# Score groups on even turns in layer 0's attention, another order and other banks in its output projection, and two weight splits per turn where the feed-forward begins

## The chip, the core and the metric

The kernel runs on one core of a Trainium2 chip. The metric is the device time of one execution in microseconds, from the first to the last instruction and what lies around them. The engines are named as in the profile: PE (TensorE, products and transposes), PEld (its weight loads), ACT (ScalarE), DVE (VectorE), POOL (GpSimd) and SP (SyncE, which issues the loads of the weights).

## What is computed

Two layers of a transformer trunk on 256 tokens of 1024 features. Layer 0 uses a dilated sliding-window attention with three head groups per head (windows 128, 512, 2048 with steps 1, 4, 16), merged by their softmax denominators; layer 1 a block-sparse attention. Each layer ends with a gated feed-forward with a causal convolution of width 3. The reference, cut:

```python
def reference(x, attn_norm, a_w_qkv, ..., ffn_w_down):
    for i in range(DEPTH):                       # 2
        hn = rmsnorm(x, attn_norm[i])
        x = x + (mixer_dilated if i % 2 == 0 else mixer_moba)(hn, w_qkv, q_gain, k_gain, w_o, cos, sin)
        hn = rmsnorm(x, ffn_norm[i])
        x = x + conv_ffn(hn, ffn_w_up[i], ffn_conv_w[i], ffn_conv_b[i], ffn_w_down[i])

def mixer_dilated(h, ...):
    qkv = h @ w_qkv                              # (256, 3 * 3 * 16 * 64)
    q, k = rope(rmsnorm(q)), rope(rmsnorm(k))
    # per head group: scores, mask, softmax, times v; then merged
    return attn @ w_o

def conv_ffn(h, w_up, conv_w, conv_b, w_down):
    u = h @ w_up                                 # (256, 2 * 2816)
    uc = conv_b + sum(conv_w[j] * shifted(u, j) for j in range(3))
    gate, val = uc[..., :D_FF], uc[..., D_FF:]
    return (silu(gate) * val) @ w_down
```

## The kernel before

**Products in three parts.** All is float32. A weight unit is loaded raw (SP), ACT copies it to a shorter type (whi, line 87) and DVE subtracts to get the rest (wlo, line 96). An activation is held in two parts likewise (xT in the profile, lines 372 and 373). A product is then three matmuls: first part times whi, second part times whi, first part times wlo (mm3, lines 384 to 386). Tokens come in two chunks of 128, c = 0 and 1. The `Stream` class holds the queue of weight units: `start` issues whi on ACT, `finish` issues wlo on DVE and the next load, `take` hands units to PE.

**Turns.** The order on each engine is the order in which the program is written, and the program is written in turns (`turn`, line 184). A turn issues up to `pump` whi on ACT, then what is due in `first`, one wlo, what is due in `pre`, the other wlo, then its piece of products for PE, then what is due in `post`. Functions enter themselves for later turns by `at(table, dt, fn)`. Pieces of a product with 12 matmuls of 512 columns make one turn in the attention.

**Attention of layer 0.** Four sections of four heads. A section has, for each of three head groups, four turns for queries and keys (two for chunk 0, then two for chunk 1), then four turns for values; sections 0 and 2 have four more for values. Turns are counted from the start of the section. A product's result sits in a bank named acc (three banks). Queries and keys are scaled, rotated and transposed back (line 473, acc<-ident,qk). The scores of two heads of one chunk are a *score group* (`step_A`, lines 573 and 582, into two banks named S); the table `plan` says after which turn of the section each group stands. One turn later DVE takes maxima with the mask (line 595) and ACT the exponentials (line 605), one more turn later DVE divides (line 615) and PE transposes the result (line 622, two banks named PT), then ACT copies it (pT, line 629) and PE multiplies with the values (line 649, one bank named O). After the second group of a chunk O is split into aT, which has the buffer name xT too (lines 372, 373). In the last section the four groups stand on turns 13 to 16, so their later steps fall into the turns of the output projection. Between islands of such small products PE runs weight products.

**Output projection** (`out_proj`, line 675). Chunk c, half n of the output columns, and weight unit u (rows 256u to 256u+255): eight units in the order `OUT_UNITS`, written (n, u). Unit u needs section u of the attention, and of the last section both chunks, since the attention's tokens are permuted. `OUT_ORDER` lists for each turn the pump, the chunk and the units. Chunk 0 accumulates in acc banks, chunk 1 in S banks:

```python
acc[c, n] = ps.tile([P, 512], F32, name="acc" if c == 0 else "S", bufs=3 - c)
```

When a half is complete it is added to the residual (line 695), squared, and with both halves the chunk's norm is computed and transposed (line 280) into the next activation.

**Feed-forward** (`ffn`, line 713). Eleven blocks of 256 columns in both halves j (gate and value). Block 0 is computed in four turns with the tokens on the partitions and transposed (line 745, into the PT banks). From block 1 on, each turn computes 128 columns of the block for both chunks (24 matmuls of 256 columns, lines 760 to 762). The convolution (`conv`) runs on ACT (line 774) and DVE (line 777); with both halves done, gate times value is split into two parts (kT, lines 786, 787), which the down-projection reads (lines 801 to 803, into the S and PT banks). From block 2 on, each second turn of j = 1 is followed by a down-projection of an earlier block.

## Time and profile before

| | us |
|---|---|
| median of 3 runs | 788.14 |
| lowest and highest run | 788.06, 788.2 |
| the profiled execution's own time | 788.0 |
| its span, first to last instruction | 786.2 |
| PE busy in it | 776.2 |
| DVE busy | 551.2 |
| ACT busy | 480.8 |

The span is 1.8 us shorter than the execution's own time. A row of a timeline has a start and a length. Lengths of PE's products overlap: the next one starts before the last has ended, so the time of a stretch of PE is read from start to start. A group of small products between weight products is called an island here.

### The profile page before, as it was taken

The numbers are of one execution on the slowest core, as the hardware profiler recorded it, in microseconds if no ns is written. First come the engines' busy times: TensorE is split into PE (matmuls) and PEld (weight loads), VectorE is DVE, ScalarE is ACT, GpSimd is POOL, SyncE is SP. The second block draws the span as 40 slices with busy tenths as digits, with TensorE's granted clock in tenths as the row PEclk, the third lists the DMA queues.
The fourth block names the chain that finished last, engine by engine and source line by source line (L and its number), as shares of the span: only waits on it lengthen the run. The fifth ranks groups of instructions, "written<-read, shape, count | busy, mean of one in ns | idle before, by whom it ended". The sixth has DMA issues, their size and how long they took to land.

```text
span 786.2 us, 13306 instructions
## 1 busy us (share of the span) xinstructions
PE 776.2 (99%) x5042; PEld 669.2 (85%) x5042; DVE 551.2 (70%) x1010; ACT 480.8 (61%) x811; POOL 89.3 (11%) x117
## 2 busy tenths in 40 slices
PE   8999999999999999999999999999999999999997
PEld 6888887888887779999999988777778999999996
DVE  6884876785686565887656777787866686676763
ACT  7677576676666546575554655877755565565550
POOL 3720331230231000000000002132100000000000
PEclk9999999999999999999999999999999999999999
DMA  9976436445356425576665563653535467556611
GB/s 292 292 241 209 123 122 188 135 141 182 114 181 214 135 81 165 167 236 209 190 208 167 161 203 120 204 169 109 158 111 183 140 208 242 167 161 193 203 34 53
DMA packets 107919, 133.89 MB, mean 170 GB/s; under 512 B 5968, under 2 KB 92368, under 8 KB 107856
## 3 DMA queue, kind: packets, MB, share of 16 engines
q1 hardware_dynamic: 107280, 130.96, 52.6%
q0 software_dynamic: 576, 2.10, 0.7%
q8 instruction: 39, 0.64, 0.3%
q14 instruction: 24, 0.20, 0.1%
HBM read 131.99 MB, written 1.05 MB: 169 GB/s over the span
## 4 chain that ended last, share of the span: by engine, by line
PE 90%; ACT 4%; DVE 3%; DMA 1%; issue 1%; SPq 0%; DVEq 0%; ACTq 0%
PE acc L384 12%; PE acc L386 12%; PE acc L385 12%; PE acc L762 9%; PE acc L761 9%; PE acc L760 9%; PE S L801 3%; PE S L802 3%; PE S L803 3%; PE PT L801 2%; PE PT L803 2%; PE PT L802 2%; PE O L649 2%; PE PT L622 2%; PE acc L473 2%; PE S L573 2%
## 5 line engine op out<-in xcount | busy, mean ns | idle before, releaser
L96 DVE TENSOR_TENSOR wlo<-raw,whi 128x1024 fp32r<-128x1024 f32 (+1 forms) x248 | 289.5, 1204 | 18.5 <-ACT whi L87 18.5
L87 ACT ACTIVATE whi<-raw 128x1024 fp32r<-128x1024 f32 (+1 forms) x248 | 249.0, 1040 | 17.6 <-PE PT L802 13.9
L384 PE MATMUL acc<-whi,xT 128*128 128x512 f32 x448 | 183.2, 409 | 2.0 <-ACT whi L87 1.3
L762 PE MATMUL acc<-xT,wlo 128*128 128x256 f32 x640 | 181.2, 283 | 0.5 <-DVE wlo L96 0.5
L760 PE MATMUL acc<-xT,whi 128*128 128x256 f32 x640 | 181.1, 283 | 0.0
L761 PE MATMUL acc<-xT,whi 128*128 128x256 f32 x640 | 181.1, 283 | 0.0
L386 PE MATMUL acc<-wlo,xT 128*128 128x512 f32 x448 | 176.0, 393 | 0.6 <-DVE wlo L96 0.5
L385 PE MATMUL acc<-whi,xT 128*128 128x512 f32 x448 | 174.9, 390 | 0.4 <-DVE xT L373 0.2
L761 PEld LDWEIGHTS acc<-xT,whi 128*128 128x128 f32 x640 | 122.7, 192 | 1.3
L760 PEld LDWEIGHTS acc<-xT,whi 128*128 128x128 f32 x640 | 122.7, 192 | 1.3
L762 PEld LDWEIGHTS acc<-xT,wlo 128*128 128x128 f32 x640 | 122.7, 192 | 0.7 <-DVE wlo L96 0.7
L777 DVE SCALAR_TENSOR_TENSOR qk<-acc,pk,qk 128x255 f32<-128x255 f32 (+1 forms) x160 | 66.1, 475 | 72.9 <-ACT qk L774 72.9
L384 PEld LDWEIGHTS acc<-whi,xT 128*128 128x128 f32 x448 | 84.1, 188 | 21.7 <-issue 2.6
L386 PEld LDWEIGHTS acc<-wlo,xT 128*128 128x128 f32 x448 | 84.0, 188 | 21.5 <-DVE wlo L96 3.0
L385 PEld LDWEIGHTS acc<-whi,xT 128*128 128x128 f32 x448 | 84.4, 188 | 16.3 <-DVE xT L373 1.0
L774 ACT ACTIVATE qk<-acc,pk 128x256 f32<-128x256 f32 x80 | 40.6, 558 | 33.0 <-PE acc L762 33.0
L263 POOL TENSOR_TENSOR rs_y<-rs_v,mhalf 128x8 f32<-128x8 f32 x32 | 53.3, 1664 | 2.7
L786 ACT ACTIVATE kT<-qk 128x512 fp32r<-128x512 f32 x22 | 13.9, 632 | 54.8 <-DVE qk L784 54.8
L261 POOL TENSOR_SCALAR rs_v<-qssq,rn_e 128x8 f32<-128x8 f32 x32 | 16.4, 513 | 217.9 <-DVE qssq L436 217.7
L780 ACT ACTIVATE qk<-qk 128x512 f32<-128x512 f32 x22 | 13.9, 633 | 35.6 <-DVE qk L777 35.6
L801 PE MATMUL S<-whi,kT 128*128 128x512 f32 x88 | 34.7, 394 | 0.0
L802 PE MATMUL S<-whi,kT 128*128 128x512 f32 x88 | 34.7, 394 | 0.0
(126 smaller groups left out, 920.0 us busy)
## 6 DMA issues: line engine op xcount, KB each, us to landing
raw<-in_ffn_w_up_dram SPq DMA_DIRECT2D x80, 512.0 KB, 4.6
raw<-in_a_w_qkv_dram SPq DMA_DIRECT2D x144, 256.0 KB, 4.2
raw<-in_ffn_w_down_dram SPq DMA_DIRECT2D x44, 512.0 KB, 5.0
raw<-in_b_w_qkv_dram SPq DMA_DIRECT2D x48, 256.0 KB, 4.0
raw<-in_a_w_o_dram SPq DMA_DIRECT2D x8, 512.0 KB, 4.1
raw<-in_ffn_w_up_dram SPq DMA_DIRECT2D x16, 256.0 KB, 5.5
raw<-in_b_w_o_dram SPq DMA_DIRECT2D x8, 512.0 KB, 3.8
xr<-in_x_t_dram SPq DMA_DIRECT2D x4, 256.0 KB, 5.5
```

Source lines behind the costliest of these rows:

```text
L87: self.nc.scalar.activation(hi[:, i], raw[:, i], AF.Copy)
L96: self.nc.vector.tensor_sub(lo[:, i], self.raw[self.done][:, i], r32(hi[:, i]))
L263: nc.gpsimd.tensor_tensor(y, v, mhalf[:, 0:n], op=ALU.pow)
L384: nc.tensor.matmul(acc, T[:, k, 0, cs], hi, start=first, stop=False)
L385: nc.tensor.matmul(acc, T[:, k, 1, cs], hi, start=False, stop=False)
L386: nc.tensor.matmul(acc, T[:, k, 0, cs], lo, start=False, stop=last)
L760: nc.tensor.matmul(o, hi[:, k % 4, es], xT[:, k, 0], start=(k == 0), stop=False)
L761: nc.tensor.matmul(o, hi[:, k % 4, es], xT[:, k, 1], start=False, stop=False)
L762: nc.tensor.matmul(o, lo[:, k % 4, es], xT[:, k, 0], start=False, stop=(k == 7))
L777: nc.vector.scalar_tensor_tensor(o[:, d:S], u[:, 0:S - d], cw[:, first_tap + b:first_tap + b + 1], o[:, d:S], op0=ALU.mult, op1=ALU.add)
L801: nc.tensor.matmul(o, acts[f][:, 0, cs], hi[:, sl], start=(b == 0), stop=False)
L802: nc.tensor.matmul(o, acts[f][:, 1, cs], hi[:, sl], start=False, stop=False)
```

## The change

Five edits. (1) In sections 0 to 2 of layer 0's attention the two score groups of chunk 0 stand after turns 14 and 18 instead of 13 and 17. (2) `OUT_ORDER` of layer 0 now names chunk and unit for each piece, so a turn may mix chunks; chunk 0's third unit moves into the second turn, and the turns behind have one unit each. (3) In both layers chunk 1's first half accumulates in an acc bank; only its second half goes to S. (4) In the last turns of layer 0's attention (after its turn 12) and in its output projection a turn's second whi is issued behind the functions due in `first` (`crowded`). (5) The turns of the feed-forward's block 1 have a pump of 2 throughout, in both layers.

```diff
-OUT_ORDER = (((1, 0, 0, 1), (1, 1, 0, 1), (2, 0, 2, 3), (0, 1, 2), (1, 0, 4, 5), (0, 0, 6), (0, 0, 7), (0, 1, 3), (1, 1, 4),
-              (1, 1, 5), (0, 1, 6), (0, 1, 7)),
-             tuple((1, 0, u) for u in range(8)) + tuple((int(u < 6), 1, u) for u in range(8)))
+OUT_ORDER = (((1, (0, 0), (0, 1)), (1, (1, 0), (1, 1), (0, 2)), (2, (0, 3)), (0, (1, 2)), (1, (0, 4)), (0, (0, 5)), (0, (0, 6)),
+              (0, (0, 7)), (0, (1, 3)), (1, (1, 4)), (1, (1, 5)), (0, (1, 6)), (0, (1, 7))),
+             tuple((1, (0, u)) for u in range(8)) + tuple((int(u < 6), (1, u)) for u in range(8)))
...
-    def turn(fn, pump=2):
+    def turn(fn, pump=2, crowded=False):
+
         t = now[0]
         end = len(ws.parts) if t >= LATE else None
-        ws.start(min(pump, 1 if len(ws.parts) - ws.taken >= AHEAD else 2))
+        n = min(pump, 1 if len(ws.parts) - ws.taken >= AHEAD else 2)
+        ws.start(min(n, 1) if crowded else n)
         for f, a in first.pop(t, ()):
             f(*a)
+        if crowded:
+            ws.start(n - 1)
         ws.finish(1, end)
...
-            plan = odd = [(13, 0, (0, 1)), (17, 0, (2, 3)), (22, 1, (0, 1)), (26, 1, (2, 3))]
+            plan = odd = [(14, 0, (0, 1)), (18, 0, (2, 3)), (22, 1, (0, 1)), (26, 1, (2, 3))]
...
-                turn(fn, pumps[i] if sec == 0 and i < len(pumps) else 2)
+                turn(fn, pumps[i] if sec == 0 and i < len(pumps) else 2, dil and sec == NSEC - 1 and i > 12)
...
-        def piece(c, *idx):
+        def piece(*idx):
             def go():
-                for n, u in idx:
+                for c, i in idx:
+                    n, u = OUT_UNITS[i]
                     if c == 0:
                         units[n, u] = ws.take(1)[0]
                     _, hi, lo = units[n, u]
                     if u == 0:
-                        acc[c, n] = ps.tile([P, 512], F32, name="acc" if c == 0 else "S", bufs=3 - c)
+                        acc[c, n] = ps.tile([P, 512], F32, name="S" if c and n else "acc", bufs=2 if c and n else 3)
...
-        for pump, c, *us in OUT_ORDER[l]:
-            turn(piece(c, *(OUT_UNITS[u] for u in us)), pump)
+        for pump, *idx in OUT_ORDER[l]:
+            turn(piece(*idx), pump, l == 0)
...
-                    turn(up(f, j, e, st), 1 if f == 1 and (j, e) != (1, 0) else 2)
+                    turn(up(f, j, e, st), 2)
```

In the changed file the functions stand four or five lines lower, so mm3 is lines 388 to 390 there, and so on. The order of the instructions shows what moves.

PE in section 0 of layer 0's attention, around the first score group (S; t are the queries and keys of the second and third head group). Before it stands alone:

```order
L386 MATMUL acc<-wlo,xT 128x512
L573 MATMUL S<-kT 128x256 x6
L582 MATMUL S<-t_505 64x64 x2
L582 MATMUL S<-t_639 64x64 x4
L582 MATMUL S<-t_505 64x64 x2
L384 MATMUL acc<-whi,xT 128x512
L385 MATMUL acc<-whi,xT 128x512
```

Now:

```order
L390 MATMUL acc<-wlo,xT 128x512
L577 MATMUL S<-kT 128x256 x6
L586 MATMUL S<-t_505 64x64 x2
L586 MATMUL S<-t_639 64x64 x4
L586 MATMUL S<-t_505 64x64 x2
L477 MATMUL acc<-ident,qk 128x128 x4
L388 MATMUL acc<-whi,xT 128x512
```

The group stands one turn later, in front of the transposes of the third head group of chunk 1. Counted over the whole program, PE has 87 islands between weight products before and 80 now; in layer 0's attention seven pairs have become one.

PE behind the last O group of layer 0 (pT_3164). acc_3028 and acc_3130 (before) or acc_3100 (now) are the two halves of chunk 0; whi_3003 is unit (0, 3), the first that needs the last section, and whi_2953 is unit (1, 2), which was whi_2940 before. Before:

```order
L386 MATMUL acc_3130<-wlo_2941,xT_180 128x512
L649 MATMUL O_3174<-pT_3164,v1_2868 64x128 x2
L649 MATMUL O_3174<-pT_3164,v2_2320 64x64 x4
L649 MATMUL O_3174<-pT_3164,v1_2968 64x128 x2
L384 MATMUL acc_3028<-whi_3003,xT_180 128x512
L385 MATMUL acc_3028<-whi_3003,xT_180 128x512
L386 MATMUL acc_3028<-wlo_3004,xT_180 128x512
```

Now:

```order
L390 MATMUL acc_3028<-wlo_2938,xT_180 128x512
L653 MATMUL O_3174<-pT_3164,v1_2868 64x128 x2
L653 MATMUL O_3174<-pT_3164,v2_2316 64x64 x4
L653 MATMUL O_3174<-pT_3164,v1_2968 64x128 x2
L388 MATMUL acc_3100<-whi_2953,xT_180 128x512
L389 MATMUL acc_3100<-whi_2953,xT_180 128x512
L390 MATMUL acc_3100<-wlo_2954,xT_180 128x512
L388 MATMUL acc_3100<-whi_2953,xT_180 128x512
L389 MATMUL acc_3100<-whi_2953,xT_180 128x512
L390 MATMUL acc_3100<-wlo_2954,xT_180 128x512
L388 MATMUL acc_3028<-whi_3003,xT_180 128x512
L389 MATMUL acc_3028<-whi_3003,xT_180 128x512
```

Unit (1, 2) of chunk 0 stood ahead of the O group and stands behind it now; the six products of chunk 0's unit (1, 0) moved from the third turn into the second in exchange.

DVE where layer 0's feed-forward begins, from the second weight parts ahead of the first convolution: the convolutions of block 0's gate (out of PT), block 1's gate (out of acc) and block 0's value (out of PT), then gate times value (qk<-qk) and its second part (kT). Before:

```order
L96 TENSOR_TENSOR wlo<-raw,whi 128x1024 x5
L777 SCALAR_TENSOR_TENSOR qk<-PT,pk,qk 128x255 x2
L777 SCALAR_TENSOR_TENSOR qk<-PT,pk,qk 128x254 x2
L96 TENSOR_TENSOR wlo<-raw,whi 128x1024
L777 SCALAR_TENSOR_TENSOR qk<-acc,pk,qk 128x255 x2
L777 SCALAR_TENSOR_TENSOR qk<-acc,pk,qk 128x254 x2
L96 TENSOR_TENSOR wlo<-raw,whi 128x1024
L777 SCALAR_TENSOR_TENSOR qk<-PT,pk,qk 128x255 x2
L777 SCALAR_TENSOR_TENSOR qk<-PT,pk,qk 128x254 x2
L784 TENSOR_TENSOR qk<-qk 128x512
L787 TENSOR_TENSOR kT<-qk,kT 128x512
L96 TENSOR_TENSOR wlo<-raw,whi 128x1024 x2
```

Now:

```order
L96 TENSOR_TENSOR wlo<-raw,whi 128x1024 x5
L782 SCALAR_TENSOR_TENSOR qk<-PT,pk,qk 128x255 x2
L782 SCALAR_TENSOR_TENSOR qk<-PT,pk,qk 128x254 x2
L96 TENSOR_TENSOR wlo<-raw,whi 128x1024 x2
L782 SCALAR_TENSOR_TENSOR qk<-acc,pk,qk 128x255 x2
L782 SCALAR_TENSOR_TENSOR qk<-acc,pk,qk 128x254 x2
L96 TENSOR_TENSOR wlo<-raw,whi 128x1024 x2
L782 SCALAR_TENSOR_TENSOR qk<-PT,pk,qk 128x255 x2
L782 SCALAR_TENSOR_TENSOR qk<-PT,pk,qk 128x254 x2
L789 TENSOR_TENSOR qk<-qk 128x512
L792 TENSOR_TENSOR kT<-qk,kT 128x512
L96 TENSOR_TENSOR wlo<-raw,whi 128x1024
```

Two second weight parts stand between the convolutions where one stood, and one behind the activations where two stood. On ACT the first parts move alike: four whi instead of two ahead of the first convolution.

## Rows read from the trace of the kernel before

**Rows 1.** The page, part 1: busy time of each engine, its share of the span, and its instructions.
```profile
PE 776.2 (99%) x5042; PEld 669.2 (85%) x5042; DVE 551.2 (70%) x1010; ACT 480.8 (61%) x811; POOL 89.3 (11%) x117
```

**Rows 2.** Busy time by stretches of the span. Columns: from and to (us), length, then for each engine busy us and instructions, and at the end the granted share of the TensorE clock, the DMA share and GB/s.
```profile
20.00:250.00 230.00, 230.00 (x1481) 186.28 (x1482) 167.30 (x342) 155.72 (x283) 58.06 (x61) 1.00 0.56 176
250.00:300.00 50.00, 48.47 (x318) 38.35 (x317) 28.82 (x50) 27.62 (x53) 1.89 (x6) 1.00 0.42 132
300.00:340.00 40.00, 39.48 (x299) 37.92 (x298) 28.81 (x43) 25.71 (x37) 0.00 (x0) 1.00 0.55 175
340.00:480.00 140.00, 140.00 (x949) 130.09 (x949) 98.29 (x137) 75.63 (x105) 1.11 (x4) 1.00 0.61 193
577.00:625.00 48.00, 48.00 (x309) 42.76 (x308) 29.83 (x42) 27.41 (x43) 1.88 (x6) 1.00 0.41 132
```

**Rows 3.** Timeline of PE in the last section of layer 0's attention and the first products of its output projection. Columns: start us, length us, engine, line, operation, output<-inputs, sizes, count, and in brackets the idle time before and what ended it. Between the second and third row shown stand a score group and its transposes; between the fourth and fifth as well.
```profile
252.52 0.39 PE L385 MATMUL acc<-whi,xT 128*128 128x512 f32 x1
252.75 0.39 PE L386 MATMUL acc<-wlo,xT 128*128 128x512 f32 x1
...
254.66 0.47 PE L384 MATMUL acc<-whi,xT 128*128 128x512 f32 x1
...
257.28 0.39 PE L386 MATMUL acc<-wlo,xT 128*128 128x512 f32 x1
...
260.08 0.50 PE L384 MATMUL S<-whi,xT 128*128 128x512 f32 x1 [0.66 <-DVE mx L595]
```

**Rows 4.** Timeline of PE around the last two O groups of that attention (16 products of O each) and the first products behind them.
```profile
270.25 0.39 PE L386 MATMUL S<-wlo,xT 128*128 128x512 f32 x1
...
271.96 0.39 PE L386 MATMUL acc<-wlo,xT 128*128 128x512 f32 x1
...
274.01 0.39 PE L386 MATMUL acc<-wlo,xT 128*128 128x512 f32 x1
274.33 0.89 PE L649 MATMUL O<-pT,v 128*64 128x128 f32 x16
275.94 0.50 PE L384 MATMUL acc<-whi,xT 128*128 128x512 f32 x1 [0.72 <-ACT xT L372]
276.59 0.50 PE L385 MATMUL acc<-whi,xT 128*128 128x512 f32 x1
276.93 0.40 PE L386 MATMUL acc<-wlo,xT 128*128 128x512 f32 x1
```

**Rows 5.** Timeline of PE at the beginning of layer 0's feed-forward: the up-projection of block 2, and the first product of the down-projection (S<-whi,kT).
```profile
318.53 0.28 PE L760 MATMUL acc<-xT,whi 128*128 128x256 f32 x1
318.65 0.28 PE L761 MATMUL acc<-xT,whi 128*128 128x256 f32 x1
319.45 0.39 PE L762 MATMUL acc<-xT,wlo 128*128 128x256 f32 x1 [0.52 <-DVE wlo L96]
319.67 0.28 PE L760 MATMUL acc<-xT,whi 128*128 128x256 f32 x1
...
320.75 0.40 PE L801 MATMUL S<-whi,kT 128*128 128x512 f32 x1
```

**Rows 6.** Timeline of DVE: the second part of the attention output (xT) behind the last O group.
```profile
275.92 0.62 DVE L373 TENSOR_TENSOR xT<-O,xT 128x256 fp32r<-128x256 f32 x1 [4.42 <-ACT xT L372]
```

**Rows 7.** Timeline of ACT, DVE and PE behind the second score group of chunk 1 in section 1, which stands on an even turn, 26 (its products begin at 164): splits, exponentials, bias (nbias), 1/sum (rd), and the transposes of sm.
```profile
166.52 2.00 ACT L87 ACTIVATE whi<-raw 128x1024 fp32r<-128x1024 f32 x2
168.41 0.61 ACT L605 ACTIVATE sm<-sm,nbias 128x384 f32<-128x384 f32 x1
167.19 0.17 DVE L599 TENSOR_SCALAR nbias<-mx 128x2 f32<-128x2 f32 x1
169.94 0.75 DVE L615 TENSOR_SCALAR sm<-sm,rd 128x384 f32<-128x384 f32 x2
171.60 0.82 PE L622 MATMUL PT<-ident,sm 128*128 128x128 f32 x6
```

**Rows 8.** Timeline of PE: the last product ahead of, and the second product behind, a score group alone (51 to 53), a block of four transposes alone (55 to 56), and both in one island (95 to 97).
```profile
51.30 0.39 PE L386 MATMUL acc<-wlo,xT 128*128 128x512 f32 x1
...
52.90 0.39 PE L385 MATMUL acc<-whi,xT 128*128 128x512 f32 x1
...
55.21 0.39 PE L386 MATMUL acc<-wlo,xT 128*128 128x512 f32 x1
...
56.11 0.40 PE L385 MATMUL acc<-whi,xT 128*128 128x512 f32 x1
...
94.95 0.39 PE L386 MATMUL acc<-wlo,xT 128*128 128x512 f32 x1
...
96.95 0.39 PE L385 MATMUL acc<-whi,xT 128*128 128x512 f32 x1
```

**Rows 9.** Timeline of ACT, then DVE, at the beginning of layer 0's feed-forward: two splits and the first convolution on ACT; the convolution of the second half (out of PT), the last part of the activations (kT) and two second weight parts on DVE.
```profile
300.08 2.00 ACT L87 ACTIVATE whi<-raw 128x1024 fp32r<-128x1024 f32 x2
302.69 1.02 ACT L774 ACTIVATE qk<-PT,pk 128x256 f32<-128x256 f32 x2 [0.60 <-PE PT L745]
314.49 1.65 DVE L777 SCALAR_TENSOR_TENSOR qk<-PT,pk,qk 128x255 f32<-128x255 f32 x4 [1.48 <-ACT qk L774]
317.57 0.69 DVE L787 TENSOR_TENSOR kT<-qk,kT 128x512 fp32r<-128x512 f32 x1 [0.70 <-ACT kT L786]
318.18 2.35 DVE L96 TENSOR_TENSOR wlo<-raw,whi 128x1024 fp32r<-128x1024 f32 x2
```

## The prediction

> **What bounds the kernel now.** I read the busy line of the page first: TensorE (PE) is busy for 99% of the span [rows 1]. So the question is not which engine is slow but where PE stands still, and how much it spends between the weight products. The table by stretches answers the first half [rows 2]: from 20 to 250 us, the whole attention of layer 0 up to its last section, PE is busy 230.00 of 230.00 us; from 250 to 300 us, the end of that attention and the output projection, it lacks 1.53 us, and from 300 to 340 us, the beginning of the feed-forward, 0.52 us. In the same two places of layer 1 (577 to 625 us) it lacks nothing. The rows of PE there name the releasers [rows 3 to 5]: DVE's row maxima (mx), ACT's copy of the attention output (xT), and DVE's second weight part (wlo). All three are places that the change touches.
>
> These idle numbers are too small. A product of 512 columns is drawn 0.39 us long, but the next one starts 0.23 us after it [rows 3], so a wait first eats the overlap before it shows as idle time. I therefore measure each place from start to start, against a twin of the same instructions that did not wait. By the idle column the three waits are 0.66 + 0.72 + 0.52 = 1.90 us [rows 3 to 5]; by starts they come to 2.88 (below). The Trainium skill (Perfetto Trace Analysis, section Tensor Engine Instruction (MATMUL, LD_WEIGHTS)) says that the end of a TensorE row is estimated from the instruction's size and not observed; counting idle time alone would give 1.90, counting starts 2.88, and these rows bear out the second.
>
> **The change part by part.** No product, transpose or transfer is added or removed, and POOL's and SP's orders stay; everything is order on PE, ACT and DVE, and banks.
>
> *Bank of chunk 1's first half.* The score group of the last heads, its neighbour transposes and then the first product into an S bank: 257.28 to 260.08, 2.80 us. The same island one turn earlier, followed by a product into an acc bank, takes 252.75 to 254.66, 1.91 us [rows 3]. The difference, **0.89 us**, is the wait for DVE to have read the scores out of that S bank. In the new order this half accumulates in the third acc bank, whose last content, a transposed block, ACT copies out two turns before. What is late next: the other half still goes to an S bank, but starts 24 products (5.5 us) later. I count the whole 0.89.
>
> *Order of the first turns.* The third product behind the last O group should start 1.71 us after the last product before the group, as it does at 270.25 to 271.96; behind the last O group it takes 274.01 to 276.93, 2.92 us [rows 4]. Cost **1.21 us**. The units that need the last section's output wait there for ACT's copy and then for DVE's difference, which ends at 275.92 + 0.62 = 276.54 [rows 6]; PE goes on at 276.59, that is 2.58 after 274.01. In the new order one unit that doesn't need it (six products, weight unit (1, 2) of chunk 0) stands between. Its third product starts at +1.71, its sixth at +2.40, and the first product that needs the copy at +2.63 instead of +1.93, the first that needs the difference at +2.86: later than 2.58 by 0.28. So all 1.21 us should go, with a thin margin. The islands ahead keep their neighbours: PT and O of the earlier groups are still separated by six or more products from their inputs, and the O bank's refill (second-last O group) has the same six products in front as before.
>
> *Splits behind the exponentials.* In the last section's late turns and in the projection the second whi of a turn moves behind the exponentials on ACT. The first effect is that one pair of exponentials starts 1.0 us earlier (one whi, half of a pair of 2.00 us [rows 7]). Nobody on PE waits for that pair once the S bank is out of the way, so I count nothing; what it covers is the thin margin above. The whi that comes later for it is first read by PE in the projection's sixth turn.
>
> *Score groups on even turns.* In sections 0 to 2 the two groups of chunk 0 move from turns 13 and 17 to 14 and 18. Nothing waits there today, so only the cost of the islands can change. From the last product before to the second product after: a score group alone 51.30 to 52.90 = 1.60, a transposed block (acc) alone 55.21 to 56.11 = 0.90, both in one island 94.95 to 96.95 = 2.00 [rows 8]. Two islands hold two product steps more, 2 x 0.23: 1.60 + 0.90 - 0.46 = 2.04, so a merged island saves about 0.05 us. The new order has 80 islands instead of 87; in five of the seven merges a score group gets a neighbour behind it. For score with O there is no row; the nearest is score with transposes. I take 7 x 0.04 = **0.3 us**; ends 0 and 0.7 (twice the row for all seven).
>
> *Two splits per turn at the feed-forward's beginning.* PE reads the second half of a weight unit at 319.45 where 318.65 + 0.12 = 318.77 was due, and the next product is another 0.10 late [rows 5]: **0.78 us**. The wlo it waits for is the first of the pair at 318.18 on DVE, queued behind the convolution at 314.49 and the gate, whose last step is at 317.57 [rows 9]. In the new order two more whi (2.00 us) stand ahead of the first convolution on ACT, which begins at 302.69 now and at 300.08 + 4.00 = 304.08 then, 1.39 us later; the wlo comes ahead of the convolution of 314.49. Even at 314.49 + 1.39 = 315.88 it would be 2.9 us early. Next in line are the activations that the first down-projection reads: their last part ends at 317.57 + 0.69 + 1.39 = 319.65 at the worst, and PE, 0.78 earlier than now, reads it at 320.75 - 0.78 + 0.23 = 320.20. The cover is 0.55 us. In layer 1 the same setting moves one whi, PE doesn't wait there today [rows 2], and I count 0 (at worst the 0.45 us by which one whi of 1.0 exceeds a cover of 0.55).
>
> **Sum.** 0.89 + 1.21 + 0.78 + 0.30 = 3.18 us. The profiled execution took 788.0 us (span 786.2 and 1.8 around it), 0.1 below the median of 788.14. From the median: 788.14 - 3.18 = 784.96, **785.0 us**, 0.40% faster. Behind these places PE is busy without a gap to 480 us [rows 2], so what is saved there is not given back.
>
> **The rivals.**
> *The last section's softmax sets the end.* If not PE but the chain maxima, exponentials, division, transposes, pT, O decides when the last O group can run, PE only waits elsewhere, and 0.89 and 1.21 stay: 788.14 - 1.08 = 787.1. For it: both waits hang on that chain. Against it: the last O group runs where its turn puts it, and its row at 274.33 shows no idle time before it [rows 4]. Chance 0.08.
>
> *The exponentials come late (slower).* On even turns both whi of the next turn stand ahead of the exponentials on ACT. The trace has that case: the bias is ready at 167.19 + 0.17 = 167.36, but two whi run from 166.52, the exponentials begin at 168.41, the division ends at 169.94 + 0.75 = 170.69, and PE's transposes of sm begin at 171.60 [rows 7], of which the 0.44 of the acc block in front (0.90 - 0.46, above) falls away in five of the six moved groups: a cover of 0.47 us. If an exponential comes later than there by x, each of six groups loses x - 0.47; from x = 1.0 (one more whi, or weights that land late) the gain is gone, from 1.3 the kernel is slower by over 0.2%, and with two whi, x = 2.0, it is 6 x 1.53 - 3.18 = 6.0 us slower: 794.1. Against it: today's even groups have this order without a wait, and DMA is at 0.56 there [rows 2]. Chance 0.06. The Trainium skill (Perfetto Trace Analysis, the same section) says that ACT and DVE are strictly first in, first out; by that rule the two whi delay each exponential, and the row at 168.41 agrees.
>
> *Banks run out.* The third acc bank is now held through the whole projection, and the norm's transposes and the feed-forward's first product share the other two. If they wait for a split on DVE once, that is some 1.2 us (two of the kind of 0.62 [rows 6]): 786.2. Against it: 12 products stand between. Chance 0.08. That the change doesn't do what it says is excluded by the order of the instructions.
>
> **How the numbers follow.** Forecast 0.78; the rivals 0.08, 0.06, 0.08. A measurement of this kernel tells about 0.2% (1.6 us) from no change, so 786.6 is the bound. Faster: forecast and the banks, 0.86. Same: the softmax chain and the mild end of the late exponentials, 0.09. Slower: 0.05. Low end: 0.7 instead of 0.3 for the islands, and the profile's 0.1: 784.4. High end: the banks' case, 786.2, and a little of partial waits, 786.4; this leaves out the softmax chain and the late exponentials, 0.14.
>
> **What would show it.** After the change PE should have no idle time ahead of the projection's first S product, of the first product behind the last O group, and of the wlo product around 316; a score group and its transposes should take 2.00 us from product to second product; the transposes of sm in sections 0 to 2 should begin 0.23 us behind a product. Waits of PE on rd or sm (L622), on an xT of the norm, or on kT in the first down-projection would be the rivals. Wrong altogether would be a wait for O's bank, or weights that land late because they are asked for earlier.

## The result: 784.1 us, 0.5% faster, and 0.9 us more than forecast

The changed kernel takes 784.08 us (median of 5 runs, 783.74 to 784.67) against 788.14 us for the kernel before in the same comparison (788.0 to 788.68): ratio 0.9949, 95% interval 0.9938 to 0.9961. That is 4.06 us; the forecast was 3.18 us, and its range ended at 784.4. The interval of the ratio reaches from 3.1 to 4.9 us, so the timing alone cannot say which term was too small. The two profiles can. The changed kernel's profiled execution took 784.07 us with a span of 782.2, before it was 788.0 and 786.2, so 4.0 us of span are to be found.

The busy line of the page of the changed kernel answers to [rows 1]: PE still sets the time.

```profile
PE 774.9 (99%) x5042; PEld 670.7 (86%) x5042; DVE 550.3 (70%) x1010; ACT 480.3 (61%) x811; POOL 89.9 (11%) x117
```

The same stretches as in [rows 2] (the last one 4 us earlier, columns as there) show that PE lacks nothing any more from 20 to 480 us:

```profile
20.00:250.00 230.00, 230.00 (x1486) 187.37 (x1486) 167.04 (x344) 155.81 (x285) 59.16 (x61) 1.00 0.57 177
250.00:300.00 50.00, 50.00 (x338) 40.57 (x337) 29.41 (x49) 30.11 (x57) 1.89 (x6) 1.00 0.46 143
300.00:340.00 40.00, 40.00 (x302) 38.48 (x301) 32.03 (x49) 25.48 (x38) 0.00 (x0) 1.00 0.60 187
340.00:480.00 140.00, 140.00 (x943) 129.69 (x942) 96.64 (x134) 76.01 (x104) 2.23 (x8) 1.00 0.58 185
573.00:621.00 48.00, 48.00 (x309) 42.76 (x308) 30.72 (x43) 28.02 (x44) 1.88 (x6) 1.00 0.46 143
```

The number of weight products on PE is the same in both kernels, so the k-th product of one can be set beside the k-th of the other, and the difference of their starts is what has been gained so far. That is how every gain below is measured. The start of the kernel is left out of it: the 121st product starts at 39.68 us before and at 39.70 after, but anywhere from 39.47 to 41.18 us in the traces of the experiments. The timeline of PE of the changed kernel at the places of [rows 3] and [rows 4]:

```profile
251.96 0.39 PE L390 MATMUL acc<-wlo,xT 128*128 128x512 f32 x1
...
253.86 0.47 PE L388 MATMUL acc<-whi,xT 128*128 128x512 f32 x1
...
256.48 0.39 PE L390 MATMUL acc<-wlo,xT 128*128 128x512 f32 x1
...
258.39 0.47 PE L388 MATMUL acc<-whi,xT 128*128 128x512 f32 x1
...
270.91 0.40 PE L390 MATMUL acc<-wlo,xT 128*128 128x512 f32 x1
271.23 0.89 PE L653 MATMUL O<-pT,v 128*64 128x128 f32 x16
272.05 0.50 PE L388 MATMUL acc<-whi,xT 128*128 128x512 f32 x1
272.39 0.40 PE L389 MATMUL acc<-whi,xT 128*128 128x512 f32 x1
272.63 0.39 PE L390 MATMUL acc<-wlo,xT 128*128 128x512 f32 x1
```

256.48 to 258.39 is 1.91 us, exactly as 251.96 to 253.86 one turn earlier, where before it was 2.80 [rows 3]. 270.91 to 272.63 is 1.72 us, where before it was 2.92 [rows 4]. The same at the beginning of the feed-forward, which answers to [rows 5]:

```profile
315.58 0.28 PE L765 MATMUL acc<-xT,whi 128*128 128x256 f32 x1
315.70 0.28 PE L766 MATMUL acc<-xT,whi 128*128 128x256 f32 x1
315.82 0.28 PE L767 MATMUL acc<-xT,wlo 128*128 128x256 f32 x1
315.94 0.28 PE L765 MATMUL acc<-xT,whi 128*128 128x256 f32 x1
...
317.02 0.40 PE L806 MATMUL S<-whi,kT 128*128 128x512 f32 x1
```

From 315.58 to 317.02 is 1.44 us, before 318.53 to 320.75 = 2.22. The account by the k-th product:

| up to | start before | start after | gained so far | in this stretch | forecast |
|---|---|---|---|---|---|
| 121st product | 39.68 | 39.70 | -0.02 | | |
| last product ahead of the score group that [rows 3] begin with | 252.75 | 251.96 | 0.79 | 0.81 | 0.30 |
| first product shown in [rows 5] | 318.53 | 315.58 | 2.95 | 2.16 | 0.89 + 1.21 = 2.10 |
| first product of the down-projection | 320.75 | 317.02 | 3.73 | 0.78 | 0.78 |
| last product of the kernel | 781.81 | 777.83 | 3.98 | 0.25 | 0 |

The waits were sized right to 0.06 us. What was missed is 0.5 us in sections 0 to 2, where only islands were moved, and 0.25 us in layer 1. The second has its row. The timeline of PE before and then after, at the first score group of layer 1's second section:

```profile
505.81 0.50 PE L573 MATMUL S<-kT,t 64*128 64x256 f32 x4 [0.46 <-DVE t L509]
```

```profile
501.81 0.50 PE L577 MATMUL S<-kT,t 64*128 64x256 f32 x4 [0.18 <-DVE t L513]
```

PE waits there in both, 0.28 us less in the changed kernel. [rows 2] leave this stretch out, so the wait of before did not show in the rows that the forecast was made from.

### The profile page after: what moved, and what is told of

The parts are those of the page before. It is cut to its first block, busy times and chain, and to the rows that moved or that the text cites. A ratio compares the mean times of both kernels' runs of the same rounds, so it can differ in the third digit from the quotient of the medians.

```text
span 782.2 us, 13324 instructions
## 1 busy us (share of the span) xinstructions
PE 774.9 (99%) x5042; PEld 670.7 (86%) x5042; DVE 550.3 (70%) x1010; ACT 480.3 (61%) x811; POOL 89.9 (11%) x117
## 4 chain that ended last, share of the span: by engine, by line
PE 96%; ACT 1%; DVE 1%; DMA 1%; issue 0%; SPq 0%; DVEq 0%; ACTq 0%
PE acc L388 14%; PE acc L390 13%; PE acc L389 13%; PE acc L767 10%; PE acc L766 10%; PE acc L765 10%; PE S L806 3%; PE S L807 3%; PE S L808 3%; PE PT L808 2%; PE PT L806 2%; PE PT L807 2%; PE O L653 2%; PE PT L626 2%; PE acc L477 2%; PE S L577 2%
## 5 line engine op out<-in xcount | busy, mean ns | idle before, releaser
L388 PE MATMUL acc<-whi,xT 128*128 128x512 f32 x464 | 189.2, 408 | 1.6 <-ACT whi L87 1.6
L390 PE MATMUL acc<-wlo,xT 128*128 128x512 f32 x464 | 182.6, 394 | 0.0
L389 PE MATMUL acc<-whi,xT 128*128 128x512 f32 x464 | 181.7, 392 | 0.2 <-DVE xT L377 0.2
L388 PEld LDWEIGHTS acc<-whi,xT 128*128 128x128 f32 x464 | 87.5, 189 | 21.6 <-issue 2.9
L390 PEld LDWEIGHTS acc<-wlo,xT 128*128 128x128 f32 x464 | 87.4, 188 | 20.6 <-DVE wlo L96 1.5
L389 PEld LDWEIGHTS acc<-whi,xT 128*128 128x128 f32 x464 | 87.8, 189 | 16.7 <-DVE xT L377 0.5
```

The source lines that it names most:

```text
L388: nc.tensor.matmul(acc, T[:, k, 0, cs], hi, start=first, stop=False)
L389: nc.tensor.matmul(acc, T[:, k, 1, cs], hi, start=False, stop=False)
L390: nc.tensor.matmul(acc, T[:, k, 0, cs], lo, start=False, stop=last)
```

## Experiments

### One part of the change at a time

Four kernels, each the kernel before with one part.

Score groups on even turns:

```
-            plan = odd = [(13, 0, (0, 1)), (17, 0, (2, 3)), (22, 1, (0, 1)), (26, 1, (2, 3))]
+            plan = odd = [(14, 0, (0, 1)), (18, 0, (2, 3)), (22, 1, (0, 1)), (26, 1, (2, 3))]
```

> The kernel before with one edit: the score groups of chunk 0 on turns 14 and 18 instead of 13 and 17. Theory A (the saving is in the islands, and it depends on what stands next to a score group: a score group right ahead of an O group saves about 0.21 us, ahead of a transposed block 0.07, other neighbours 0.01 to 0.02): the first product behind the last merged island comes 0.79 us earlier, the two waits at the projection stay at 0.93 and 1.21, and the time is 788.1 - 0.8 = 787.3. Theory B (every merge saves the 0.05 of the row for scores with transposes, as forecast, and the rest of the 0.79 seen there in the changed kernel comes from another edit): 0.3 us, 787.8.

The bank of chunk 1's first half (and no other line):

```
-                        acc[c, n] = ps.tile([P, 512], F32, name="acc" if c == 0 else "S", bufs=3 - c)
+                        acc[c, n] = ps.tile([P, 512], F32, name="S" if c and n else "acc", bufs=2 if c and n else 3)
```

> The kernel before with one edit: chunk 1's first half of the output projection accumulates in the third acc bank. Theory A (waits on separate chains): the wait of 0.9 us ahead of the first S product goes, the wait behind the last O group stays at 1.2, time 788.1 - 0.9 = 787.2. Theory B (the chain of the last section's softmax, not PE, sets when the copy xT is ready): PE comes 0.9 earlier to the same xT, the wait behind the last O group grows to 2.1, time 788.1.

The order of the output projection's first turns, with the banks, splits and turns of before (the table OUT_ORDER of the changed kernel, and the loop that reads it):

```
+OUT_ORDER = (((1, (0, 0), (0, 1)), (1, (1, 0), (1, 1), (0, 2)), (2, (0, 3)), (0, (1, 2)), (1, (0, 4)), (0, (0, 5)), (0, (0, 6)),
...
+                for c, i in idx:
+                    n, u = OUT_UNITS[i]
...
+        for pump, *idx in OUT_ORDER[l]:
+            turn(piece(*idx), pump)
```

> The kernel before with one edit: the new order of the output projection's first turns, with chunk 1 in S banks as before, one split rule and the old turns. Theory A: the S wait of 0.9 us stays where the first product into S is issued, the wait behind the last O group falls from 1.2 to under 0.1, time 788.1 - 1.2 = 786.9. Theory B (the unit that was put in between is not enough, because two whi still stand ahead of the last exponentials on ACT): the first product that reads xT still waits, by up to 0.7 us, time 787.4 to 787.6.

Two splits per turn at the feed-forward's beginning:

```
-                    turn(up(f, j, e, st), 1 if f == 1 and (j, e) != (1, 0) else 2)
+                    turn(up(f, j, e, st), 2)
```

> The kernel before with one edit: two splits per turn at the feed-forward's beginning, in both layers. Theory A: the wait for wlo at 319 us (0.78) goes and nothing else moves on PE in layer 0, time 788.1 - 0.8 = 787.3; the wait of 0.5 us for t in layer 1 (at 505 us), which is 0.25 shorter in the changed kernel, is not tied to this edit or to any other: it is as long as the time by which ACT's table load starts after the bias is ready, 0.36 us in one trace and 0.07 in the other. Theory B: the 0.25 in layer 1 belongs to this edit, since it alone changes the splits ahead of that place: 787.1, with the table load 0.07 us after the bias.

| kernel | gained on PE, by the trace | time, us | before, us | ratio, 95% interval |
|---|---|---|---|---|
| even turns alone | 0.81 in layer 0, 0.28 in layer 1 | 786.95 | 788.09 | 0.9987 [0.9978, 0.9996] |
| bank alone | 0.26 | 787.84 | 788.09 | 0.9998 [0.9989, 1.0007] |
| order alone | 1.25 | 786.88 | 788.09 | 0.9985 [0.9976, 0.9993] |
| two splits alone | 0.78 in layer 0, 0.28 in layer 1 | 787.04 | 788.09 | 0.9986 [0.9977, 0.9995] |

The even turns give 0.81 us by themselves (theory A), the two splits exactly 0.78. The order alone gives its 1.21 and a little (theory A): from the last product ahead of the last O group to the third behind it PE takes 1.72 us, where before it was 2.92 [rows 4].

```profile
272.40 0.40 PE L390 MATMUL acc<-wlo,xT 128*128 128x512 f32 x1
...
274.12 0.39 PE L390 MATMUL acc<-wlo,xT 128*128 128x512 f32 x1
```

The bank alone gives next to nothing, and not for the reason of theory B. The timeline of PE of the kernel with the bank alone, the last product ahead of the transposes of the third group of heads, the transposes, the O group and the next product:

```profile
262.05 0.39 PE L386 MATMUL acc<-wlo,xT 128*128 128x512 f32 x1
262.92 0.87 PE L622 MATMUL PT<-ident,sm 128*128 128x128 f32 x6 [0.48 <-ACT pT L629]
263.73 0.89 PE L649 MATMUL O<-pT,v 128*64 128x128 f32 x16
264.55 0.50 PE L384 MATMUL acc<-whi,xT 128*128 128x512 f32 x1
```

The S wait of 0.9 us is gone, but one turn later PE waits 262.92 - 262.05 - 0.23 = 0.64 us for ACT's copy pT, and the next product starts at 264.55, where before it was 264.52. (The start of this kernel took 0.24 us longer, which is why that counts as a gain of 0.2 us and not as none.) The wait behind the last O group is as it was. ACT's timeline of the same kernel shows why the copy is late:

```profile
261.08 0.62 ACT L605 ACTIVATE sm<-sm,nbias 128x384 f32<-128x384 f32 x1 [1.18 <-DVE nbias L599]
...
262.29 0.85 ACT L629 ACTIVATE pT<-PT 128x512 f32<-128x512 f32 x2
```

The copy that frees the PT banks stands behind the exponentials of the next group, and ACT stands still for 1.18 us ahead of those, waiting for the bias. The Trainium skill (Perfetto Trace Analysis, section Tensor Engine Instruction (MATMUL, LD_WEIGHTS)) says that ACT is strictly first in, first out; the rows agree, since the transposes that the copy reads had ended before 260 us (they start at 258.80 and are drawn 0.88 us long).

So bank and order are not two terms. Alone they give 0.26 and 1.25 us, together 2.16: the new order puts six more products (1.4 us) ahead of those transposes, and only behind this cover does the bank pay.

### Is it the copy?

To show that the copy's place on ACT is the cause, the bank edit was run with the copy pT ahead of the exponentials of the next group, for the two groups where both stand in one turn; PE, DVE, POOL and SP keep the order of the bank edit:

```
-        for f, a in first.pop(t, ()):
+        for f, a in sorted(first.pop(t, ()), key=lambda e: 69 < t < 76 and e[0].__name__ == "step_E"):
...
-            at(pre, 1, step_V, sec, c, heads, v, Tp, tot)
+            at(first if dil and sec == NSEC - 1 and now[0] < 74 else pre, 1, step_V, sec, c, heads, v, Tp, tot)
```

> The kernel before with the bank edit, and on ACT, in the last section, the copy pT of one group of heads ahead of the exponentials of the next group instead of behind them (the order on PE, DVE, POOL and SP is that of the bank edit alone). Theory A (the wait that took the place of the S wait is for the two PT banks: their copy stands on ACT behind exponentials that ACT itself waits 1.2 us for): the wait of 0.64 us ahead of the transposes at 262 us goes, PE keeps the whole 0.9 us of the bank edit, the wait behind the last O group stays at 1.2; 788.1 - 0.9 = 787.2. Theory B (those transposes wait for their operand sm all the same): wait as with the bank alone, 787.8.

The timeline of PE, from the last product ahead of the transposes on, and of ACT in that kernel:

```profile
261.81 0.40 PE L386 MATMUL acc<-wlo,xT 128*128 128x512 f32 x1
262.04 0.82 PE L622 MATMUL PT<-ident,sm 128*128 128x128 f32 x6
262.79 0.89 PE L649 MATMUL O<-pT,v 128*64 128x128 f32 x16
```

```profile
259.47 0.86 ACT L629 ACTIVATE pT<-PT 128x512 f32<-128x512 f32 x2
260.86 0.62 ACT L605 ACTIVATE sm<-sm,nbias 128x384 f32<-128x384 f32 x1 [0.52 <-DVE nbias L599]
```

The wait is gone: the transposes start 0.23 us behind the product, and PE is 0.91 us ahead behind them. Of this 0.79 us are left at the end of the kernel; the rest is lost in steps of 0.05 us and less. The time is 787.51 us against 788.10 (ratio 0.9994 [0.9985, 1.0003]), an interval in which both 0.9 us and nothing lie, so the trace and not the time decides here. Theory A holds.

### What the split rule is worth

The rule that puts a turn's second whi behind the exponentials was taken out of the changed kernel, and, apart from that, added to the bank edit:

```
-                turn(fn, pumps[i] if sec == 0 and i < len(pumps) else 2, dil and sec == NSEC - 1 and i > 12)
+                turn(fn, pumps[i] if sec == 0 and i < len(pumps) else 2, False)
...
-            turn(piece(*idx), pump, l == 0)
+            turn(piece(*idx), pump)
```

> The changed kernel with one part undone: both splits of a turn again ahead of the exponentials, in the last section and the projection. Theory A (the six more products that the new order puts ahead of the transposes of the last heads are cover enough; the split rule is worth nothing here, as forecast): no wait on PE at 262 us, time as the changed kernel, 784.1. Theory B (without it the last heads' maxima on DVE and with them the copies pT come 0.3 to 0.5 us later and PE waits for them again): 784.4 to 784.6.

```
-    def turn(fn, pump=2):
+    def turn(fn, pump=2, crowded=False):
...
-        ws.start(min(pump, 1 if len(ws.parts) - ws.taken >= AHEAD else 2))
+        n = min(pump, 1 if len(ws.parts) - ws.taken >= AHEAD else 2)
+        ws.start(min(n, 1) if crowded else n)
         for f, a in first.pop(t, ()):
             f(*a)
+        if crowded:
+            ws.start(n - 1)
```

> The kernel before with two edits: the bank of chunk 1's first half, and the split rule of the last section and the projection; the old order of the turns. With the bank alone PE waited 0.64 us, start to start, ahead of the transposes of the last heads, for ACT's copy pT. Theory A (that copy hangs on exponentials that hang on DVE's maxima, which hang on the exponentials two groups earlier; the split rule moves one whi of 1.0 us out of their way): the maxima come 0.48 us earlier, a wait of 0.16 remains, PE is 0.45 to 0.5 us further than with the bank alone, time 787.3. Theory B (the split rule changes nothing that PE waits for, because ACT stood idle for 1.2 us ahead of the last exponentials anyway): wait 0.64 as before, time 787.8.

Without the rule the changed kernel takes 784.35 us (ratio to before 0.9947 [0.9935, 0.9960], with it 0.9949), and no product past the start moves by more than 0.04 us in one turn. With the bank edit the rule leaves the wait for pT at 0.63 us and the time at 787.84 us (0.9995 [0.9986, 1.0004]). So theory B holds for the second, not theory A: the last maxima wait for PE's scores and for two wlo on DVE, not for the exponentials that the rule moves ahead. The rule is worth nothing here, as the prediction had it.

### What a merge of islands is worth

The changed kernel with the second score group of chunk 0 back on its old turn:

```
-            plan = odd = [(14, 0, (0, 1)), (18, 0, (2, 3)), (22, 1, (0, 1)), (26, 1, (2, 3))]
+            plan = odd = [(14, 0, (0, 1)), (17, 0, (2, 3)), (22, 1, (0, 1)), (26, 1, (2, 3))]
```

> The changed kernel with the second score group of chunk 0 back on turn 17 (the first stays on 14): four merges of islands are undone, one in section 0 and one in section 2 (score group right ahead of an O group), two in section 1 (a transposed block with transposes of sm; O behind a score group and a block). Theory A (the saving depends on the neighbour): PE falls back by 0.21 us in section 0, 0.03 in section 1, 0.21 in section 2, against the changed kernel. Theory B (every merge saves the same, 0.79 over seven): 0.11, 0.23, 0.11.

The changed kernel with another order within an island:

```
-        for f, a in post.pop(t, ()):
+        for f, a in sorted(post.pop(t, ()), key=lambda e: t < 69 and e[0].__name__ == "transpose"):
```

> The changed kernel with one more edit: in layer 0, up to the last section, the block of projection transposes of a turn is issued on PE behind the scores and the O group, not between or ahead of them; the number of islands stays. Two score groups of section 1 so come right ahead of their O group. Theory A (what saves is a score group directly ahead of an O group): these two islands cost 0.13 us less each, all others within 0.03. Theory B (only the number of islands counts): no change on PE. A rival on the other side: the blocks come up to 1.2 us later to ACT, which copies them, and a later score group waits for them; then the products behind are later by what is missing.

With turn 17, PE falls back by 0.22 us in section 0, 0.07 in section 1 and 0.22 in section 2: much nearer to theory A (0.21, 0.03, 0.21) than to equal prices (0.11, 0.23, 0.11). (Its one run took 786.15 us, with the 121st product 1.48 us later than in the changed kernel.) With the blocks last, the two islands in which a score group now stands right ahead of O cost 0.2 us less each (0.13 was expected), so the neighbour it is. But the rival on the other side took more than that back. The block comes 1.5 us later, ACT's copy of it delays the exponentials behind it, and PE waits for the division, as the timeline of PE of that kernel shows:

```profile
156.72 0.39 PE L390 MATMUL acc<-wlo,xT 128*128 128x512 f32 x1
157.97 0.88 PE L626 MATMUL PT<-ident,sm 128*128 128x128 f32 x6 [0.87 <-DVE sm L619]
```

By starts that is 1.0 us, and 0.5 us at the second such place; from its start on the kernel loses 1.0 us against the changed one (one run, 785.33 us).

The rows from which the price could have been had stand in the trace of before. An O group alone, from the last product ahead to the second product behind:

```profile
77.32 0.39 PE L386 MATMUL acc<-wlo,xT 128*128 128x512 f32 x1
77.64 1.56 PE L649 MATMUL O<-pT,v 128*64 128x128 f32 x32
79.13 0.50 PE L384 MATMUL acc<-whi,xT 128*128 128x512 f32 x1
79.46 0.40 PE L385 MATMUL acc<-whi,xT 128*128 128x512 f32 x1
```

and the score group with O behind it, in the changed kernel:

```profile
79.95 0.39 PE L390 MATMUL acc<-wlo,xT 128*128 128x512 f32 x1
80.27 0.62 PE L577 MATMUL S<-kT 64*128 64x256 f32 x6
80.82 0.47 PE L586 MATMUL S<-t 64*64 64x64 f32 x16
81.22 1.56 PE L653 MATMUL O<-pT,v 128*64 128x128 f32 x32
82.71 0.50 PE L388 MATMUL acc<-whi,xT 128*128 128x512 f32 x1
83.05 0.40 PE L389 MATMUL acc<-whi,xT 128*128 128x512 f32 x1
```

Alone they take 1.60 [rows 8] and 2.14 us, less two product steps of 0.23 is 3.28; together they take 3.10. The steps at the edges are longer than the usual 0.23 us: 0.32 from a product to O (77.32 to 77.64), 0.33 from the first product behind it to the second (79.13 to 79.46). A merge of a score group with O saves one exit and one entrance, each about 0.1 us. A block of transposes is entered without such a price (55.21 to 55.44 us in the trace of before, 0.23), so a merge with it saves less: 0.05 [rows 8].

Priced like this, from the last product ahead to the second behind, the two merges of a score group with O save 0.20 us each and the other five 0.17 together: 0.57 of the 0.81 us. The rest lies in the products behind an island. The ten steps behind its second product are 0.230 us on average instead of 0.227 (both traces, 60 to 245 us), 0.034 us for each island, and seven islands less make 0.24. By these two prices the four merges that turn 17 undoes are worth 0.23, 0.08 and 0.23 us by section; measured were 0.22, 0.07 and 0.22.

### Layer 1: 0.28 us that hang on a place in the program

The wait for t is part of a chain that begins with the load of the exponential's table on ACT. The row of ACT before, and after:

```profile
500.39 1.28 ACT L605 ACT_TABLE_LOAD   x1 [0.57 <-DVE nbias L602]
```

```profile
496.39 1.28 ACT L609 ACT_TABLE_LOAD   x1 [0.31 <-DVE nbias L606]
```

The wait of the load ends at 500.08 before and at 496.36 after, but the load begins 0.308 us behind that before and 0.029 after. Over the traces the first went with the kernel before, bank alone and order alone, the second with even turns alone and two splits alone, which have nothing in common there. What they share is that their program for ACT is longer ahead of this place (by the instructions that signal and wait): in the trace the load is ACT's 704th instruction in the first group, and the 708th to 714th in the second. So four tiny copies were put at the start of ACT's program in the kernel before:

```
+    for i in range(4):
+        nc.scalar.activation(pad[:, P + i:P + i + 1], ident[:, i:i + 1], AF.Copy)
```

> The kernel before with four tiny copies (128x1) more at the start of ACT's program, and nothing else. Ten traces so far: in four the load of the exponential's table ahead of layer 1's first exponentials begins 0.308 us after its wait has ended, in six 0.029 us; in the four it is the same place in ACT's program, in the six it stands 4 to 10 instructions later. Theory A (the place in the program decides, not what the edits do to the work): 0.029 here, and PE's island at 505 us costs 1.59 instead of 1.87, 0.28 less. Theory B (it is tied to what the even turns or the two splits do): 0.308 and 1.87 as before. At the start of the kernel up to 0.4 us can be lost.

The rows of ACT, and of PE, in that kernel:

```profile
500.82 1.28 ACT L605 ACT_TABLE_LOAD   x1 [0.30 <-DVE nbias L602]
```

```profile
506.24 0.50 PE L573 MATMUL S<-kT,t 64*128 64x256 f32 x4 [0.18 <-DVE t L509]
```

The load begins 0.029 us behind its wait, and PE's wait is 0.18 us as in the changed kernel, although nothing of the change is in this one. So the 0.25 us belong to no edit as such: a few instructions more in ACT's program ahead of this place were enough to bring them. (The one run took 788.46 us all the same, since its 121st product came at 40.34 us instead of 39.68.)

### Going further

Two kernels tried to beat the changed one. The first moves layer 1's second section onto the turns of its neighbours:

```
-            plan, odd, last = ([(s, 0, (0, 1, 2, 3)), (s + 2, 1, (0, 1)), (s + 4, 1, (2, 3))] for s in (6, 5, 7))
+            plan, odd, last = ([(s, 0, (0, 1, 2, 3)), (s + 2, 1, (0, 1)), (s + 4, 1, (2, 3))] for s in (6, 6, 7))
```

> The changed kernel with one more edit: in layer 1 the score groups of the second section start on turn 6, as in the first, not on turn 5, so that its islands fall on the turns of its neighbours: 75 islands instead of 80. Theory A (fewer islands, each merge worth 0.05 to 0.2 us): 0.3 to 0.7 us faster than the changed kernel, 783.4 to 783.8. Theory B (two score groups now stand in one island and share two S banks, so the second waits for DVE to have read the first, and softmax work that was spread comes together): a wait of 0.5 to 2 us at 530 to 545 us, 784.5 to 786.

It takes 796.80 us: ratio to before 1.0111 [1.0098, 1.0125]. The first two merges saved 0.13 us together, and then PE waits, as the view of PE's waits in layer 1 says:

```profile
PE O L653 <- DVE xT L377: 5.3, 1, 5.3
PE S L571 <- DVE mx L599: 3.2, 1, 3.2
```

The second row comes first, at 541 us, and is theory B, larger than I had it. The first row, at 567 us, is the single O bank: two O groups now stand in one island, and the second needs the bank that the first has filled. In each wait the TensorE clock fell. The busy time by stretches shows it for the first of them (columns as in [rows 2]):

```profile
536.00:540.00 4.00, 1.63 (x11) 0.98 (x9) 3.45 (x11) 1.39 (x3) 2.10 (x2) 1.00 0.56 204
540.00:542.00 2.00, 1.14 (x8) 1.17 (x8) 1.22 (x6) 0.00 (x0) 0.00 (x0) 0.51 0.49 187
542.00:544.00 2.00, 2.00 (x11) 1.60 (x9) 0.00 (x0) 0.58 (x2) 0.00 (x0) 0.50 0.20 75
```

The second reverses the order of two steps on DVE in layer 1, for the wait of 0.18 us that is left at 501.81:

```
-            for hi, lo, src, scale in subs:
+            for hi, lo, src, scale in subs if dil else subs[::-1]:
```

> The changed kernel with one more edit: in layer 1, DVE computes the second part of a section's queries (t) ahead of that of its keys (kT), in the order in which the score products read them; nothing else moves. In the changed kernel PE still waits at 501 us for t (0.46 us, start to start, against the same island without a wait: 1.60 and 1.14). Theory A (both wait for DVE alone, and PE needs t first, kT two products later): t is there 0.45 us earlier, kT 0.4 later, the third pair of products starts 0.2 us earlier than now, the island costs 1.40, time 0.2 us less than the changed kernel, 783.9. Theory B (t waits for ACT's copy rather than for DVE's turn): no change at that island, 784.1; and a later group whose kT comes last now could wait.

PE gains 0.12 us at that island (from the last product ahead to the second behind 1.93 us instead of 2.05), and nothing waits later. The time is 784.05 us, ratio to before 0.9946 [0.9933, 0.9960]: as fast as the changed kernel, as far as it can be measured. No version was found that is faster than the change by more than that.

## Why the forecast fell short

The waits that were to go have gone, no rival came in the changed kernel, and the signs that were to show it are there: no idle time at the three places, 2.00 us for a score group with its transposes (54.04 to 56.04), and transposes of sm that start 0.23 us behind a product in sections 0 to 2. Three steps deserve to be named.

*"I take 7 x 0.04 = 0.3 us; ends 0 and 0.7"* is the step that failed. It measured 0.81, beyond its own upper end. I priced all merges by the only merged pair with a score group that before showed, scores with transposes, and took twice that row as the bound. The bound for a score group with O had to come from what a merge takes away, the edges of the islands, and those had rows in before: about 0.1 us each for a group of scores or O. The two merges with O save 0.20 us each at the island, the other five 0.17 together, which is about my price for them. Left out altogether was the third part, the products behind an island: 0.24 us for seven islands less.

*"In layer 1 ... I count 0."* The edit does nothing to the work there, which was right. The 0.25 us came from the place of an instruction in ACT's program, which I had not thought of, and which moved with edits that have nothing in common. For the forecast that is luck. The trace of before shows the wait (0.46 us of idle time at 505.81), but not that it would shrink; a small allowance to both sides for waits that depend on nothing in the change would have covered it.

*"I count the whole 0.89"* and *"all 1.21 us should go"* came to 2.10 against 2.16 measured, but for the bank the reason was incomplete. I named the acc bank's last content and the other half as late next, and wrote of the exponentials that nobody on PE waits for them once the S bank is out of the way. The copy pT stands behind them on ACT, and PE waits for it: alone the bank gives 0.26 us. The unit put in between, which I counted only behind the last O group, is also what covers that copy. The sum was right because both edits came together, and that was luck, since I had not seen that the one needs the other.

With these, 3.18 + 0.51 + 0.25 + 0.06 = 4.00 us, and the span is 4.0 us shorter. Without layer 1 it is 3.75 us, which gives 784.4, the very end of the range; the 0.25 us that belong to no edit carried the time past it.

Of what was counted at nothing or as a risk: the split rule is worth nothing (784.35 without it). The exponentials behind two whi delayed nobody in sections 0 to 2: the kernel with the even turns alone gains 0.81 us there and shows no new wait. The banks did not run out.

## What to carry to other kernels

Measure a wait from start to start against a twin that did not wait, and price a moved group by the edges that it loses or gains, each with its own neighbour, and by the products behind it, not by the one merged pair that happens to be in the trace. When an edit removes a wait, ask on every engine what stands in the queue behind the next instruction that waits, since the next wait may be for a copy there; try such an edit alone before its gain is added to others. Fewer islands are not better as such: where merged groups share a bank, the wait can be many times what the merge saves (3.2 and 5.3 us here, against 0.2 at most).

## What the runs showed that was not expected

- A load of the activation table begins 0.029 us or 0.308 us behind the end of its wait, and which of the two goes with its place in ACT's program: 0.308 in all five traces in which it is ACT's 704th instruction, 0.029 in all nine in which it stands 4 or more later, one of them with four tiny copies as the only difference. In the nine, an 8 KB packet of the instruction queue starts 1.9 to 3.6 us ahead of the load; in the five the next one starts 1.7 to 2.8 us behind it. That the loading of code is the cause is likely by this, but was not shown.
- In the kernel that took 796.80 us, PE stood still for 3.2 us up to 540.9. The granted clock fell to 0.50 (1.2 GHz) at 540.0 and rose again at 546.9; in the wait of 5.3 us up to 567.1 it fell at 563.9 and rose at 570.7. PE's weight products at this clock start 0.43 us apart (569.17, 569.60, 570.02) instead of 0.23. The waits in the middle of the other kernels, at most 0.87 us of idle time, left it at 1.00. So a long wait costs more than its length: the two together are 8.5 us, and the kernel lost 12.5 us against the changed one.
- Going from a product of 512 columns to an O or a score group and back costs about 0.1 us at each edge, and the ten steps behind the second product behind an island another 0.034 us together. No idle time in the trace shows either.
